# TensorE's queue in the order of the program text, in a kernel for one hybrid mixer and MLP layer

## The chip, the cores and the metric

The kernel runs on one core of one Trainium2 chip. Time is device time in microseconds (us) of one launch; the table below has the median of three runs, and the time of the one execution that the profiler recorded. The engines are TensorE (PE; its weight loads have their own row, PEld), VectorE (DVE), ScalarE (ACT), GpSimd (POOL) and SyncE (SP), which issues the DMAs. Each engine has a queue of its own and waits on semaphores of the others.

## What is computed

One layer on 2048 tokens of width 1024, in float32. Cut to what matters here:

```python
def hybrid_layer(x, ...):
    h = rmsnorm(x, norm_mix_w)
    proj = jnp.einsum("btd,dc->btc", h, w_in)              # 1024 -> 5648 columns
    u_b, u_c, u_h, z, xbc, dt_raw = jnp.split(proj, SPLITS, axis=-1)
    y_a = u_b * causal_dwconv(u_c * u_h, short_conv_w)     # short convolution mixer
    y_b = ssd_mixer(z, xbc, dt_raw, ...)                   # softplus(dt), chunked scan, gate, grouped rmsnorm
    x = x + jnp.einsum("btc,cd->btd", concat([y_a, y_b]), w_out)   # 2048 -> 1024
    h = rmsnorm(x, norm_mlp_w)
    hid = jnp.square(jax.nn.relu(jnp.einsum("btd,df->btf", h, w_up)))   # 1024 -> 4096
    return x + jnp.einsum("btf,fd->btd", hid, w_down)      # 4096 -> 1024
# and a last rmsnorm
```

In the scan, `dt` (16 heads) becomes a softplus, a cumulative sum over a chunk and exponentials of it; each chunk's output needs the state left by the chunk before.

## The kernel before

**Tiles.** Tokens lie on the free axis in blocks of 512 (`TB`), features on the 128 partitions; two blocks make a half. A float32 matmul is done as three matmuls on a high and a low part: `whi` and `wlo` of the weights, `uh` and `ul` of the data (L113 to L115 in `mm3`; L276 to L278 in `Seven.chain`). `Seven.chain` multiplies a 2 by 2 block of matrices with seven products in place of eight; the products accumulate in the PSUM banks `px`, `py` and `pw`, and between them ACT and DVE evict the banks (L727, L730, L874) and form the high and low parts of later data and weights (L100 and L101 for weights; L205, L206, L347 and L348 for data).

**Stages.** Norm and input projection of half 0, then half 1 with the scan of half 0 in between, then the output projection with the scan of half 1 in between, then the MLP up and down, then the last norm.

- `Rstd`: `reduce` sums squares with one-column matmuls into `pst` (L132), `root` makes the reciprocal root and two diagonals on ACT and DVE (L152), `spread` broadcasts them with two matmuls into `prb` (L178). The sums come from DVE (`facc`: L492 for the input norm, L1492 for the MLP's norm, L1079 for the last).
- `dt_part(b)` for block `b` (0 to 3): 16 or more matmuls `pd` (L625), an ACT copy `dts` (L629), four transposes `pt` (L633), then a chain of small DVE operations on 128x64 from L635 to L656 (with one ACT exponential), then two matmuls `pc` (L662, L663), a DVE copy (L664), a transpose `pr` (L671) and stores. The chain is, in its core:

```python
three(v) <- sum of pt; + bias; e = exp(-|v|)               # L635, L642, L643, L644
d = 1 / (e + 2); e = e * d; d = e * e; p = d / 17          # L646 to L650
for n in (15, 13, 11, 9, 7, 5, 3):
    nc.vector.scalar_tensor_tensor(out=p, in0=p, scalar=1.0 / n, in1=d, op0=ALU.add, op1=ALU.mult)
... L653, L655, L656: e = dt * a
```

- `Scan`: `load` brings a chunk's tiles (L1213 `dd`, L1218 `bc`, L1220 `xd`, L1222 `dec`), `front` transposes them (`ptx` L1253, `ptb` L1255 and L1256) and makes decays on ACT (L1267, L1268) and DVE (L1275), `back` does the matmuls `yo` (L1287), `st` (L1289), `yd` (L1292) and, later, a norm `pss` (L1317). `run` is a generator whose steps are interleaved with the products of the stage around it.
- `Output`: the output projection with `mm3`, 32 units; it adds the residual (L1478) and squares for the next norm (L1491, L1492).
- `Mlp`: up (evictions L871 to L878, the results go to DRAM by L861), then down, whose accumulators `acc` are loaded from DRAM (L978) and added to on DVE (L1018).

**What sets the order.** The kernel is written as one text. A scheduler runs over it ahead of the launch: it plays the program with estimated durations, and each engine takes of its instructions that are ready the one that it prefers. What comes out is a fixed list for each engine, and on the chip each engine works through its list in order, each instruction waiting for its semaphores. So an instruction that the text has early can stand later in an engine's list, and others ahead of it.

## Time and profile before

| | |
|---|---|
| median of 3 runs | 2664.36 us (2661.9 to 2666.43) |
| profiled execution | 2658.11 us |
| its span (first to last instruction) | 2656.4 us |
| DVE, ACT, POOL busy in it | 71%, 54%, 6% |
| DMA | 536.96 MB, mean 202 GB/s |
| mean granted TensorE clock | 0.995 |

A row of the page's first part gives an engine's busy time, its share of the span and its instructions. A row of the stretches gives for a window the busy time and, after x, the number of instructions of PE, PEld, DVE, ACT and POOL, then the granted TensorE clock, the DMA share and GB/s. A row of the timeline has start, duration, engine, line, operation, output and inputs, shapes and the number of like instructions that follow one another; at its end, in brackets, the idle time before it and what ended it. A row with a DMA and no start gives the tile, the number of transfers, their size and the time from issue to landing. Matmuls of 512 columns overlap: the distance of two starts tells more than the duration in their rows.

### The profile page before, as it was taken

How to read it: one execution, taken by the hardware profiler on the slowest of the kernel's cores; microseconds unless marked ns; L12 is line 12 of the kernel's file. 1: busy time of each engine (PE TensorE's matmuls, PEld its weight loads, DVE VectorE, ACT ScalarE, POOL GpSimd, SP SyncE). 2: the span in 40 equal slices, each digit the busy share in tenths (PEclk: the TensorE clock that was granted, in tenths of full speed). 3: DMA queues.
4: the chain of work that ended last, by engine and by line, in shares of the span. 5: the costliest groups of instructions: out<-in, count | busy, mean ns of one | idle time of the engine just before them, and what ended most of it. 6: DMA issues, size and time to landing. Idle time of an engine off the chain costs nothing.

```text
span 2656.4 us, 33528 instructions
## 1 busy us (share of the span) xinstructions
PE 2602.2 (98%) x12024; PEld 2124.8 (80%) x12024; DVE 1874.3 (71%) x2524; ACT 1436.5 (54%) x2178; POOL 146.1 (6%) x162
## 2 busy tenths in 40 slices
PE   7999999999999999998999999999999999999998
PEld 5788888778877888776888888888887888888887
DVE  7977867667667666666678675744447877888985
ACT  6654345766567566857336555755555434444443
POOL 0010000111111001111000000000000000000001
PEclk9999999999999999999999999999999999999999
DMA  3545735555555578867566786765558554665762
GB/s 145 196 174 182 278 143 202 182 152 174 169 161 168 165 262 267 254 200 232 193 208 214 258 315 254 258 234 178 209 183 297 155 152 153 206 219 165 249 209 71
DMA packets 292871, 536.96 MB, mean 202 GB/s; under 512 B 26208, under 2 KB 141920, under 8 KB 292704
## 3 DMA queue, kind: packets, MB, share of 16 engines
q1 hardware_dynamic: 292704, 534.82, 60.9%
q8 instruction: 94, 1.54, 0.2%
q14 instruction: 73, 0.60, 0.1%
HBM read 354.89 MB, written 179.83 MB: 201 GB/s over the span
## 4 chain that ended last, share of the span: by engine, by line
PE 59%; issue 26%; ACT 5%; DMA 4%; DVE 4%; POOL 1%; SPq 0%; POOLq 0%; DVEq 0%; ACTq 0%
PE px L276 9%; PE px L277 9%; PE px L278 9%; PE py L276 4%; PE py L277 4%; PE py L278 4%; PE pm L113 4%; PE pm L114 4%; PE pm L115 3%; PE pw L276 2%; PE pw L277 2%; PE pw L278 2%; ACT whi L100 1%; ACT dec L1267 1%; DMA dec<-rd_d 1%
## 5 line engine op out<-in xcount | busy, mean ns | idle before, releaser
L276 PE MATMUL px<-uh,whi 128*128 128x512 f32 x1672 | 657.7, 393 | 6.8 <-DVE acc L1018 1.8
L278 PE MATMUL px<-uh,wlo 128*128 128x512 f32 x1672 | 652.2, 390 | 0.0
L277 PE MATMUL px<-ul,whi 128*128 128x512 f32 x1672 | 651.9, 390 | 0.0
L276 PEld LDWEIGHTS px<-uh,whi 128*128 128x128 f32 x1672 | 314.5, 188 | 82.2 <-DVE acc L1018 3.2
L101 DVE TENSOR_TENSOR wlo<-wraw,whi 128x1024 fp32r<-128x1024 f32 x214 | 223.2, 1043 | 222.2 <-ACT whi L100 216.4
L278 PEld LDWEIGHTS px<-uh,wlo 128*128 128x128 f32 x1672 | 314.4, 188 | 66.4 <-issue 0.2
L277 PEld LDWEIGHTS px<-ul,whi 128*128 128x128 f32 x1672 | 314.6, 188 | 63.5
L100 ACT CAST whi<-wraw 128x1024 fp32r<-128x1024 f32 x214 | 193.6, 905 | 302.5 <-PE px L277 223.4
L276 PE MATMUL py<-uh,whi 128*128 128x512 f32 x836 | 327.4, 392 | 4.4 <-DVE acc L1018 3.4
L100 ACT CAST whi<-s 128x1024 fp32r<-128x1024 f32 x210 | 219.7, 1046 | 206.8 <-PE py L277 81.8
L277 PE MATMUL py<-ul,whi 128*128 128x512 f32 x836 | 325.6, 389 | 0.0
L278 PE MATMUL py<-uh,wlo 128*128 128x512 f32 x836 | 325.4, 389 | 0.0
L101 DVE TENSOR_TENSOR wlo<-s,whi 128x1024 fp32r<-128x1024 f32 x210 | 255.2, 1216 | 79.9 <-ACT whi L100 78.1
L113 PE MATMUL pm<-uh,whi 128*128 128x512 f32 (+1 forms) x648 | 253.1, 392 | 2.1 <-ACT uh L205 2.1
L114 PE MATMUL pm<-ul,whi 128*128 128x512 f32 (+1 forms) x648 | 249.9, 386 | 0.0
L115 PE MATMUL pm<-uh,wlo 128*128 128x512 f32 (+1 forms) x648 | 249.5, 385 | 0.0
L276 PEld LDWEIGHTS py<-uh,whi 128*128 128x128 f32 x836 | 156.9, 188 | 39.8 <-DVE acc L1018 3.8
L278 PEld LDWEIGHTS py<-uh,wlo 128*128 128x128 f32 x836 | 156.9, 188 | 33.0 <-DVE wlo L101 0.2
L277 PEld LDWEIGHTS py<-ul,whi 128*128 128x128 f32 x836 | 157.0, 188 | 32.0
L276 PE MATMUL pw<-uh,whi 128*128 128x512 f32 x418 | 163.5, 391 | 0.7 <-ACT pw L283 0.7
L347 ACT CAST uh<-rh 128x1024 fp32r<-128x1024 f32 (+1 forms) x128 | 120.3, 943 | 80.4 <-PE py L278 62.4
L278 PE MATMUL pw<-uh,wlo 128*128 128x512 f32 x418 | 162.9, 390 | 0.0
(232 smaller groups left out, 3763.2 us busy)
## 6 DMA issues: line engine op xcount, KB each, us to landing
hid_d<-e SPq DMA_DIRECT2D x96, 512.0 KB, 3.9
rh<-hid_d SPq DMA_DIRECT2D x96, 512.0 KB, 4.4
wraw<-w_in SPq DMA_DIRECT2D x68, 512.0 KB, 3.9
wraw<-w_down SPq DMA_DIRECT2D x104, 256.0 KB, 3.7
wraw<-w_up SPq DMA_DIRECT2D x48, 512.0 KB, 4.5
dec<-rd_d SPq DMA_DIRECT2D x32, 512.0 KB, 5.8
wraw<-w_out SPq DMA_DIRECT2D x32, 512.0 KB, 5.1
x_d<-xt SPq DMA_DIRECT2D x64, 256.0 KB, 3.2
```

Source lines behind the costliest of these rows:

```text
L100: nc.scalar.copy(hi, raw)
L101: eng.tensor_tensor(out=lo, in0=raw, in1=hi.bitcast(F32), op=ALU.subtract)
L113: nc.tensor.matmul(out, whi, hi, start=(k == 0), stop=False)
L114: nc.tensor.matmul(out, whi, lo, start=False, stop=False)
L115: nc.tensor.matmul(out, wlo, hi, start=False, stop=(k == nk - 1))
L276: nc.tensor.matmul(p, hi, h[0], start=not seeded and k == 0, stop=False, **kw)
L277: nc.tensor.matmul(p, hi, h[1], start=False, stop=False, **kw)
L278: nc.tensor.matmul(p, lo, h[0], start=False, stop=(k == len(g) - 1), **kw)
L347: nc.scalar.copy(p[i][0], t)
L1267: nc.scalar.activation(dec[:, i], dec[:, i], AF.Relu, bias=t["a"][:, i : i + 1], scale=-1.0)
```

## The change

The whole of `trunk` is traced in a context that keeps the instructions of the named engine in the order of the text. The other engines are still ordered by the scheduler, which now plays them against TensorE's fixed list.

```diff
     with tile.TileContext(nc) as tc:
-        trunk(tc, *args, out)
+        with tc.manual_schedule(engines={mybir.EngineType.PE}):
+            trunk(tc, *args, out)
```

No instruction is added or taken away. TensorE has 11512 instructions in both; 809 stand at another place, by up to 95 places, in 26 small stretches. The lists of DVE, ACT and SyncE change as well; GpSimd's is the same. Buffer numbers in tile names differ by two between the kernels.

First place, on TensorE: the matmuls of `dt_part(0)`, in the norm of block 1. `pd`, `pt`, `pc` and `pr` are those named above, `pm` the products of the input projection that follow. Before:

```order
L625 MATMUL pd<-uh_294,wdt 32x512
L625 MATMUL pd<-ul_295,wdt 32x512
L113 MATMUL pm<-uh_409,whi 128x512
L114 MATMUL pm<-ul_410,whi 128x512
L115 MATMUL pm<-uh_409,wlo 128x512
L113 MATMUL pm<-uh_409,whi 128x512
L633 MATMUL pt<-ident,dts 128x32 x4
L114 MATMUL pm<-ul_410,whi 128x512
L115 MATMUL pm<-uh_409,wlo 128x512
```

and 84 rows behind this `pt`:

```order
L113 MATMUL pm<-uh_469,whi 128x512
L662 MATMUL pc<-dts,tri 128x64
L663 MATMUL pc<-dts,ones_r 128x64
L114 MATMUL pm<-ul_470,whi 128x512
L115 MATMUL pm<-uh_469,wlo 128x512
L113 MATMUL pm<-uh_477,whi 128x512
L671 MATMUL pr<-ident,dts 64x128
```

After:

```order
L625 MATMUL pd<-uh_296,wdt 32x512
L625 MATMUL pd<-ul_297,wdt 32x512
L633 MATMUL pt<-ident,dts 128x32 x4
L662 MATMUL pc<-dts,tri 128x64
L663 MATMUL pc<-dts,ones_r 128x64
L671 MATMUL pr<-ident,dts 64x128
L113 MATMUL pm<-uh_411,whi 128x512
L114 MATMUL pm<-ul_412,whi 128x512
```

The four kinds stand directly behind one another, and the products that stood between `pt` and `pc` come behind `pr`. For block 1 it is the same: in the list of before 92 rows stand between its `pt` and its `pc`, in that of after none.

Second place, on TensorE: the first transposes of the scan (`ptx`, `ptb`), in the input projection of half 1; `px`, `py` are products of a pair of columns, `yo` the first matmuls of the chunk's `back`. Before:

```order
L276 MATMUL py<-uh_3717,whi 128x512
L1287 MATMUL yo<-bc,state_3777 128x128 x3
L1253 MATMUL ptx<-ident,xd 128x128 x4
L1255 MATMUL ptb<-ident,bc 128x128
L1256 MATMUL ptb<-bc 128x128
L1287 MATMUL yo<-bc,state_3777 128x128
L277 MATMUL py<-ul_3718,whi 128x512
```

After:

```order
L278 MATMUL py<-uh_3605,wlo 128x512
L1253 MATMUL ptx<-ident,xd 128x128 x4
L1255 MATMUL ptb<-ident,bc 128x128
L1256 MATMUL ptb<-bc 128x128
L276 MATMUL px<-uh_3655,whi 128x512
L277 MATMUL px<-ul_3656,whi 128x512
L278 MATMUL px<-uh_3655,wlo 128x512
```

The transposes moved ahead by 38 rows, from the middle of the next pair to its beginning. The scan's second start, in `Output`, has the same move by 30 rows.

Third place, on SyncE: the loads of that first chunk. `a` is a part of a weight (`a22` in `pairs`, L309), `rdt` the weights of dt. Before:

```order
L599 DMA rdt<-w_dt 128x128
L309 DMA a_3908<-w_in 128x512
L1213 DMA dd<-dt_d_105 128x256
L1218 DMA bc<-xs_d_97 128x128 x2
L1220 DMA xd<-xs_d_97 128x4x128
L1222 DMA dec<-rd_d_109 128x8x128
```

After:

```order
L599 DMA rdt<-w_dt 128x128
L1213 DMA dd<-dt_d_107 128x256
L1218 DMA bc<-xs_d_99 128x128 x2
L1220 DMA xd<-xs_d_99 128x4x128
L1222 DMA dec<-rd_d_111 128x8x128
L1243 DMA y<-sz_d_101 128x4x128
```

The load of `a` went behind the chunk's loads. At the scan's second start SyncE's list is the same in both.

## The prediction, made before the changed kernel ran

> **What bounds the kernel now.** I read the page first, then the stretches of 100 us, then the timeline at the places where the order of TensorE's instructions differs.
>
> ```profile
> PE 2602.2 (98%) x12024; PEld 2124.8 (80%) x12024; DVE 1874.3 (71%) x2524; ACT 1436.5 (54%) x2178; POOL 146.1 (6%) x162
> ```
>
> PE is busy for 2602.2 of 2656.4 us; DVE, the next engine, for 71%. A busy share can hide slow matmuls, so the number of matmuls per stretch matters too:
>
> ```profile
> 100.00:200.00 100.00, 100.00 (x443) 82.75 (x442) 78.89 (x94) 50.13 (x63) 9.40 (x12) 1.00 0.49 178
> 1200.00:1300.00 100.00, 91.72 (x456) 73.76 (x455) 62.83 (x94) 56.80 (x108) 12.23 (x9) 0.95 0.66 198
> 2000.00:2100.00 100.00, 93.17 (x398) 75.00 (x397) 81.86 (x108) 46.34 (x60) 0.00 (x0) 0.98 0.72 236
> ```
>
> The first row is the usual one: 443 matmuls in 100 us, one every 0.226 us, with no gap. PE idles visibly in few stretches; the two others shown lose 8 and 7 us. Hence two things: the same PE work can hardly run faster, since the unused time of PE is 2656.4 - 2602.2 = 54 us in all, the start and the tail included; and whatever makes PE wait anew is paid in full, because no other engine sets the end.
>
> **How I price a moved instruction.** The change keeps PE's work and moves 809 of its 11512 instructions, in small stretches. PE runs its queue in order, so a waiting instruction holds everything behind it. For each moved instruction I take from the trace of before (a) the time at which PE reached the place that the instruction now has (its slot), and (b) the time at which the last thing that it waits for was done. (b) minus (a), less a gap of before that vanishes there, is the new stall. It is a first-order figure: the other engines go on during a stall, which makes later stalls shorter, and their lists change too.
>
> **Start, +4.7.** The sum over block 1's squares (pst, L132) moves 27 places ahead.
>
> ```profile
> 32.55 0.39 PE L113 MATMUL pm<-uh,whi 128*128 128x512 f32 x1
> 33.98 3.08 DVE L492 TENSOR_TENSOR facc<-facc,sq 128x512 f32<-128x512 f32 x4
> ```
>
> Its slot is 32.55; DVE's last addition ends at 33.98 + 3.08 = 37.06. That is 4.5, and I put 0.2 on the broadcast (prb) behind it, whose chain over ACT and DVE now has only nine matmuls of cover. Bounds 2 and 6.
>
> **The dt chains, +35.6.** This is the largest term. In dt_part, pt, pc and pr are joined by a chain of 21 small DVE instructions (L635 to L656). The text gives PE nothing between pt and pc for blocks 0 and 1; the list of before puts 85 and 92 rows there.
>
> ```profile
> 50.26 0.43 PE L633 MATMUL pt<-ident,dts 32*128 32x32 f32 x4
> 53.75 0.28 DVE L635 TENSOR_REDUCE dts<-pt 128x64 f32<-128x128 f32 x1
> 69.20 0.22 DVE L656 TENSOR_TENSOR dts<-dts,hb 128x64 f32<-128x64 f32 x1
> 70.93 0.27 PE L671 MATMUL pr<-ident,dts 128*64 128x128 f32 x1
> ...
> 76.35 0.50 PE L276 MATMUL px<-uh,whi 128*128 128x512 f32 x1
> 85.02 0.68 DVE L209 TENSOR_TENSOR s<-wraw 128x512 f32<-128x512 f32 x1
> 85.62 0.54 DVE L647 RECIPROCAL dts<-dts 128x64 f32<-128x64 f32 x1
> 97.11 0.21 DVE L656 TENSOR_TENSOR dts<-dts,hb 128x64 f32<-128x64 f32 x1
> ...
> 523.77 0.39 PE L276 MATMUL py<-uh,whi 128*128 128x512 f32 x1
> 532.38 0.23 DVE L655 SCALAR_TENSOR_TENSOR dts<-dts 128x64 f32<-128x64 f32 x1
> 532.64 0.23 DVE L656 TENSOR_TENSOR dts<-dts,hb 128x64 f32<-128x64 f32 x1
> 533.01 0.41 PE L662 MATMUL pc<-dts,tri 128*128 128x64 f32 x2 [1.60 <-DVE dts L656]
> ```
>
> Block 0: PE is through with pt at 50.7 and pr could start at 70.93, so if DVE repeats itself PE stands still for 20.2. Bare, the chain takes 21 times 0.26 (the distance of the rows at 532.38 and 532.64) plus 0.3 for the longer reciprocal, 5.8, and with the hops to pt, pc and pr (about 1.5) 7.3. DVE's list of after still has 19 wide operations between L635 and L656 (21 before) at 0.60 each (85.02 to 85.62): 1.2 less than before; I take another 1.4 off since DVE should reach L635 earlier. That gives 17.6; bounds 7 and 20. Block 1: the list of after has six wide operations left inside the chain, so 5.8 + 6 x 0.60 = 9.4, and with the hops 11. If DVE is as late as before it is 97.32 - 76.35 = 21 plus 0.6 for pr; bounds 7 and 21.6. Block 3: pc's slot is 523.77, its release 532.87, less the gap of 1.99 that before has there (1.60 of it shown in the row): +7.0, bounds 3 and 9.
>
> **The scan's two starts, +13.9.** The transposes of the first chunk (ptx) stand ahead of a pair's products in the text, and some forty (first) and thirty (second) rows later in the list of before.
>
> ```profile
> 467.03 0.39 PE L276 MATMUL px<-uh,whi 128*128 128x512 f32 x1
> 473.54 0.50 PE L276 MATMUL px<-uh,whi 128*128 128x512 f32 x1 [0.91 <-ACT s L727]
> 473.91 0.43 SPq L1220 DMA_DIRECT2D xd<-xs_d  x1
> xd<-xs_d SPq DMA_DIRECT2D x1, 256.0 KB, 3.1
> ...
> 973.99 0.39 PE L113 MATMUL pm<-uh,whi 128*128 128x512 f32 x1
> 976.55 0.43 SPq L1220 DMA_DIRECT2D xd<-xs_d  x1
> xd<-xs_d SPq DMA_DIRECT2D x1, 256.0 KB, 5.5
> ```
>
> First start: slot 467.03, load landed at 473.91 + 3.1 = 477.0, so 10 late. But SyncE's list of after puts this load ahead of the weight load a22 (L309) that held it up in before, and it can be issued some 4.5 earlier: 5.4. The next products wait for an ACT eviction (L727) that now stands behind the chunk's eight decays: +2.6, less the 1.9 of gaps here that go (the wait at 473.54 among them): 6.0, bounds 2 and 12. Second start: slot 973.99, landing 976.55 + 5.5 = 982.05; SyncE's order is the same. 8.1 and 0.4 for the slower issue behind a store, less a gap of 0.6: +7.9, bounds 4 and 9.
>
> **Accumulator and eviction waits, +11.1.** Three places where the list of before has other products ahead of a waiting one, and the text has not.
>
> ```profile
> 1235.18 0.39 PE L113 MATMUL pm<-uh,whi 128*128 128x512 f32 x1
> 1242.68 0.69 DVE L1492 TENSOR_TENSOR facc<-sq,facc 128x512 f32<-128x512 f32 x1 [1.27 <-ACT sq L1491]
> 1243.42 0.80 PE L1317 MATMUL pss<-ssq,ones_r 128*128 128x128 f32 x2 [5.37 <-DVE facc L1492]
> ...
> 2008.69 0.39 PE L276 MATMUL px<-uh,whi 128*128 128x512 f32 x1
> 2012.37 0.68 DVE L874 TENSOR_TENSOR e<-py,s 128x512 f32<-128x512 f32 x1
> ...
> 2023.32 0.39 PE L276 MATMUL px<-uh,whi 128*128 128x512 f32 x1
> 2034.05 0.50 PE L276 MATMUL py<-uh,whi 128*128 128x512 f32 x1 [3.38 <-DVE acc L1018]
> 2034.93 0.69 DVE L1018 TENSOR_TENSOR acc<-px,acc 128x512 f32<-128x512 f32 x1 [0.94 <-DMA acc<-x_d]
> ```
>
> pss (L1317) stands 12 matmuls earlier, ahead of the same late release: 12 x 0.226 = +2.7. px at 2008.69 waits for an eviction (L874) that ended at 2012.45, 3.8 late, of which before lost 1.1: +2.7. At 2023.32 the text wants the next product, whose bank DVE frees at 2034.93 + 0.69 = 2035.62; before ran 25 later matmuls in that time, 25 x 0.226 = +5.7, work that is still to do when the bank comes free. Bounds of the three: 4 and 19.
>
> **Tail, +4.5.** The final norm's sums (pst) are asked for before their squares are added:
>
> ```profile
> 2621.44 0.28 PE L113 MATMUL pm<-uh,whi 128*128 128x256 f32 x1
> 2622.25 0.68 DVE L1079 TENSOR_TENSOR facc<-facc,sq 128x512 f32<-128x512 f32 x1
> ```
>
> Slot 2621.44, release 2622.93: 1.5; about as much for the broadcast behind it, and 1.5 for the same pair in the second half. Bounds 2 and 6.
>
> **Smaller places, +7.** Eight more moves (the dt of block 2, and single evictions) come out 0.4 to 2 us late each in the same way; an estimate, bounds 3 and 9.
>
> **The clock after a stall, +8.4.** PE does not resume at full rate:
>
> ```profile
> 1219.30 0.33 PE L1255 MATMUL ptb<-ident,bc 128*128 128x128 f32 x1 [2.92 <-DVE state L1303]
> 1220.37 0.63 PE L115 MATMUL pm<-uh,wlo 128*128 128x512 f32 x1
> ...
> 1245.94 0.63 PE L114 MATMUL pm<-ul,whi 128*128 128x512 f32 x1
> 1246.37 0.63 PE L115 MATMUL pm<-uh,wlo 128*128 128x512 f32 x1
> ```
>
> After the idle 5.37 us that end at 1243.42, matmuls start 0.43 apart in place of 0.226, and for about 3.8 us; a pause of 2.92 was enough for the same (0.63 at 1220.37). About seven matmuls at 0.20 more are 1.4 us; six of the stalls above are long enough and have no slow clock behind them in before (start, dt of blocks 0, 1 and 3, both scan starts): 8.4. Bounds 5 and 12.
>
> [...]
>
> **Sum.** 4.7 + 35.6 + 13.9 + 11.1 + 4.5 + 7 + 8.4 = 85.2. The profiled execution took 2658.1 (span 2656.4), so that one would become 2743. The runs shown have their median 6.3 above it, at 2664.4; I add the same and forecast **2750**.
>
> **The rivals.** (1) *The other engines use the stalls.* While PE stands still, DVE, ACT and the loads go on, so each stall shortens those behind it, and the chains run bare. Then each term sits at its lower bound: 2 + 7 + 7 + 3 + 2 + 4 + 4 + 2 + 3 + 5 = 39, **2703**. For it: DVE is idle 29% of the time. Against it: at dt of block 0 the wide operations are inside DVE's list, and DVE can't skip them.
> (2) *Nothing is absorbed.* Each term at its upper bound: 6 + 20 + 21.6 + 9 + 12 + 9 + 19 + 6 + 9 + 12 = 124, **2788**. For it: the new DVE and ACT lists were laid out against estimated durations, and what is late there holds PE again. Against it: 21.6 at block 1 needs wide operations that no longer stand in the chain.
> (3) *Faster: the text waits less than the list.* PE's own gaps in before are waits of instructions that the list put too early, 3.38 at 2034.05 for example. If text order moved these waits behind their releases, at the very most the 54 us that PE is unused could come back; with the bare chains of blocks 0 and 1 (14.6) still to pay, 2664 - 54 + 15 = **2625**. It decides only if more than 20 us of gaps go (the 14.6 and the 5 that can be told from none); at the three places shown the text moves the waiting instruction earlier, not later, which speaks against it.
> (4) *No difference.* 93% of PE's instructions keep their place; if all moved ones were ready, **2664**. Against it stand the 85 rows between pt and pc, which the text takes away.
>
> **How the numbers follow.** Forecast 0.60 (2720 to 2775), rival 1 0.20, rival 2 0.14, rivals 3 and 4 0.03 each. The range 2700 to 2785 leaves out rivals 3 and 4, most of rival 2 and the lower part of rival 1. A difference of 0.2%, 5 us, is about the least that a measurement of this kernel can tell from none. Faster by more: 0.03 (rival 3); within: 0.03 (rival 4); slower: 0.94 (the rest).
>
> **What would show it.** In the profile of the changed kernel the largest waits of PE should be pc for L656, 11 to 18 us each in the first 130 us, and the first stretch of 100 us should hold well under 300 matmuls (in before its row has x362); ptx should wait for xd at 470 and 980 of the old time, 5 and 8 us; px for L1018 once for over 8 us at the start of the down phase. The granted clock should dip behind each. If PE's wait for L656 in block 0 is under 9, rival 1 holds; if block 1's is over 18, rival 2. I am wrong in kind if the difference lies outside these places: if the list of DVE or ACT has PE wait a little in each of the many repeated steps, or if the dt waits are gone.

## The result, and the profile after

The changed kernel takes 2744.96 us (median of 4 runs, 2740.56 to 2746.54) where the kernel before, run beside it, takes 2664.0: a ratio of 1.0302 (95% interval 1.0286 to 1.0318), 81 us slower. Its profiled execution took 2740.56 us, 82.5 more than that of before. The forecast was 2750.

The page of the kernel after, its row of TensorE:

```profile
PE 2619.4 (96%) x12024; PEld 2137.8 (78%) x12024; DVE 1879.8 (69%) x2524; ACT 1436.4 (52%) x2176; POOL 141.2 (5%) x162
```

The span grew by 2738.9 - 2656.4 = 82.5 us. PE's busy time grew by 17.2 with the same instructions, its idle time by 65.3: most of the loss is waiting, and some is matmuls that ran slower. The stretches of 100 us of the kernel after (busy time and, after x, instructions of PE, PEld, DVE, ACT, POOL; then the granted clock, DMA share, GB/s) show where:

```profile
0.00:100.00 100.00, 63.85 (x248) 48.56 (x249) 71.36 (x136) 55.75 (x82) 2.86 (x11) 0.88 0.37 132
100.00:200.00 100.00, 90.83 (x399) 74.82 (x398) 67.34 (x97) 43.13 (x58) 6.33 (x8) 0.95 0.42 145
300.00:400.00 100.00, 100.00 (x443) 82.81 (x442) 79.96 (x98) 41.71 (x53) 7.87 (x12) 1.00 0.68 242
500.00:600.00 100.00, 82.14 (x387) 62.26 (x386) 57.97 (x108) 61.29 (x107) 5.86 (x9) 0.91 0.46 143
1000.00:1100.00 100.00, 90.92 (x444) 73.87 (x443) 62.13 (x89) 62.30 (x125) 8.82 (x6) 0.95 0.86 277
```

Three stretches are thinned that are full or nearly so in before: the first 120 us, 500 to 600 and 1000 to 1100 (the thin ones around 1300 and 2100 are there in before too, 65 to 75 us earlier). Between them (300 to 400 as the example) PE runs as before, 443 matmuls in 100 us. The waits of PE name the causes (waiter and what it waited for; us in all, times, the longest):

```profile
PE pc L662 <- DVE dts L656: 32.4, 3, 14.5
PE ptx L1253 <- DMA xd<-xs_d: 17.3, 3, 9.1
PE pst L132 <- DVE facc L492: 16.0, 2, 12.3
PE px L276 <- DVE acc L1018: 11.1, 10, 5.9
PE pss L1317 <- DVE facc L1492: 8.5, 1, 8.5
...
PE px L276 <- DVE e L874: 4.0, 1, 4.0
PE px L276 <- DVE eb L730: 3.7, 2, 1.9
```

The same view of before had 2.2 for pc, 0.6 for ptx, 12.7 for pst (block 0's, which the start needs in both) and 5.4 for pss. The dt of block 0 in the timeline of after:

```profile
57.89 0.40 PE L633 MATMUL pt<-ident,dts 32*128 32x32 f32 x4 [1.27 <-ACT dts L629]
58.34 0.29 DVE L635 TENSOR_REDUCE dts<-pt 128x64 f32<-128x128 f32 x1
72.43 0.23 DVE L656 TENSOR_TENSOR dts<-dts,hb 128x64 f32<-128x64 f32 x1
72.81 0.66 PE L662 MATMUL pc<-dts,tri 128*128 128x64 f32 x2 [14.52 <-DVE dts L656]
74.28 0.42 PE L671 MATMUL pr<-ident,dts 128*64 128x128 f32 x1 [0.39 <-DVE dts L664]
74.92 0.63 PE L114 MATMUL pm<-ul,whi 128*128 128x512 f32 x1
75.35 0.63 PE L115 MATMUL pm<-uh,wlo 128*128 128x512 f32 x1
...
112.12 0.77 PE L276 MATMUL px<-uh,whi 128*128 128x512 f32 x1
```

PE stands still from 58.3 to 72.8 while DVE works through the chain, then runs matmuls 0.43 apart. The first px behind dt of block 1 starts at 112.12; in before it started at 76.35. By that matmul the kernel has lost 35.8 us. Read in this way, start against start of one matmul in both timelines, the two executions drift apart by the steps in this table. The slow clock behind each wait is part of the drift, so the forecast's 1.4 for it is added at the six places where it was counted.

| place | forecast | drift |
|---|---|---|
| start, pst of block 1 | 4.7 + 1.4 | 7.2 |
| dt of block 0 | 17.6 + 1.4 | 18.1 |
| dt of block 1 | 11 + 1.4 | 10.7 |
| scan, first start | 6.0 + 1.4 | 7.8 |
| dt of block 3 | 7.0 + 1.4 | 8.2 |
| scan, second start | 7.9 + 1.4 | 11.2 |
| pss in the output projection | 2.7 | 4.1 |
| end of up, start of down | 2.7 + 5.7 | 6.2 |
| last norm | 4.5 | 2.4 |
| all the rest | 7 | 6.5 |
| sum | 85.2 | 82.4 |

### The profile page after: what moved, and what is told of

Its sections match the earlier page's. It is cut to its first block, busy times and chain, and to the rows that moved or that the text cites. A ratio compares the mean times of both kernels' runs of the same rounds, so it can differ in the third digit from the quotient of the medians.

```text
span 2738.9 us, 33543 instructions
## 1 busy us (share of the span) xinstructions
PE 2619.4 (96%) x12024; PEld 2137.8 (78%) x12024; DVE 1879.8 (69%) x2524; ACT 1436.4 (52%) x2176; POOL 141.2 (5%) x162
## 4 chain that ended last, share of the span: by engine, by line
PE 57%; issue 26%; DVE 6%; DMA 5%; ACT 4%; POOL 1%; SPq 0%; POOLq 0%; DVEq 0%; ACTq 0%
PE px L276 9%; PE px L277 9%; PE px L278 8%; PE py L276 4%; PE py L277 4%; PE py L278 4%; PE pm L113 3%; PE pm L114 3%; PE pm L115 3%; PE pw L276 2%; PE pw L278 2%; PE pw L277 2%; DMA dec<-rd_d 2%; ACT whi L100 1%; PE yd L1292 1%
## 5 line engine op out<-in xcount | busy, mean ns | idle before, releaser
L277 PE MATMUL pw<-ul,whi 128*128 128x512 f32 x418 | 162.7, 389 | 0.0
```

The lines of the kernel that those rows point to most:

```text
L277: nc.tensor.matmul(p, hi, h[1], start=False, stop=False, **kw)
```

## The experiments

My theory: the loss is made place by place, by single instructions at the head of PE's queue that are not ready, each with a stall and a slow clock behind it. The rivals: the loss comes from the new lists of the other engines over the whole kernel; or waits that are taken away come back elsewhere. All ratios below are against the kernel before, run beside each kernel.

### Text order in some stages only

For these three the whole-kernel context goes, and `text_order()` is the same context, put around stages.

```diff
-            ws = proj.start()
+            with text_order(): ws = proj.start()
```

> TensorE in text order only while the first stage (norms, first blocks of the projection, dt of blocks 0 and 1) is traced; the scheduler orders it in the rest. Theory (the loss is made place by place, by waits at the head of TensorE's queue): the two profiles drift apart by 7.2 us up to the first dt matmul and by 18.1 more at dt of block 0; at dt of block 1 the region ends, so products of the next stage may stand between pt and pc (36 rows, 8.1 us of the 9.8 us wait). 7.2 + 18.1 + 2 = 27 us above before: 2691 us. Rival (the loss comes from the other engines' lists, which change over the whole kernel): within 10 us of before, or as slow as a proportional share of the whole, under 2680 us.

Measured: 2688.79 us, 26.6 above before (2662.18), ratio 1.0097 (1.0082 to 1.0112); pc of block 0 waits 14.5 as in the whole change.

The complement has the same context around `first_half`, `second_half`, the loops over the output's units, and the MLP, and not around `start`.

> The complement: TensorE in text order in every stage but the first. Theory: what the profiles drift apart behind the first stage, 82.4 - 36.1 = 46 us: 2710 us, with the waits for xd (8 and 9 us), pc of block 3 (9.5) and pss (9) as in the changed kernel and no wait for L656 in the first 130 us. Rival (not additive, an early stall gives the other engines a lead that hides later ones): clearly more than 46 us.

Measured: 2706.08 us, 43.9 above before, ratio 1.016 (1.0145 to 1.0175). Both sizes are as the drift says. Their sum is 26.6 + 43.9 = 70.5; with the 8 us of block 1's pc that neither kernel has, it comes near the whole 81. The loss adds up over stages.

```diff
+    with text_order():
+        with tc.tile_pool(name="up", ...) as mlp.up:
             ...
+        mlp.down(c4, ws)
```

> TensorE in text order only in the MLP's up and down and the last norm. Theory: 82.4 - 68.5 = 14 us: 2678 us, most of it at the end of the up phase (px waiting for L874) and in the last norm. Rival (the small differences in the down phase are noise or come from earlier stages): 8 us or less, 2672 us.

Measured: 2672.1 us, 9.9 above before, ratio 1.0036 (1.0024 to 1.0048): between the two, nearer the rival. Some 4 us of the 14 that I had put down to the MLP are not made there when it alone is in text order; by the interval it is 1 to 8.

### What the slow clock costs

```diff
+    def fill_wait(bank, n):
+        for _ in range(n):
+            k = bank.shape[-1] // P
+            out = bank.rearrange("p (k c) -> p k c", k=k)
+            nc.tensor.matmul(out, ones_r, ones_r.unsqueeze(1).to_broadcast([P, k, P]), start=True, stop=True)
...
             pc = psum("tp", "pc", 2)
+            fill_wait(pc[:, 128:512], (74, 42, 0, 44)[b])
```

> The changed kernel with matmuls on constants, whose results nobody reads, ahead of five waiting instructions: 74, 42 and 44 of 384 columns ahead of pc of blocks 0, 1 and 3, 28 and 34 of 512 columns ahead of the first ptx of the scan's two halves. They end before the wait does, so TensorE is busy in place of idle. Theory (a pause of some 3 us or more halves the clock for about 4 us, 1.4 to 1.9 us lost each): five slow stretches less, 7 to 9 us below the changed kernel, 2737 us, with the granted clock at full in these places. Rival (the slow stretch costs nothing, since TensorE then waits for less): no difference, 2745 us; rival (the added matmuls delay the waiting ones): above 2748 us.

The kernel also had 10 such matmuls ahead of block 1's pst, a sixth place that the expectation does not count. Measured: 2733.72 us, ratio 1.0272 (1.0252 to 1.0293) against 1.0302 (1.0286 to 1.0318) for the change: 232 matmuls more, and some 8 us less. The intervals overlap a little, so the size is loose; the profiled executions lie 6.7 us apart. The stretches behind the waits, first of the changed kernel (dt of block 0, dt of block 3, second start of the scan):

```profile
72.00:78.00 6.00, 4.81 (x16) 3.90 (x17) 3.14 (x9) 1.84 (x4) 0.00 (x0) 0.58 0.47 129
580.00:586.00 6.00, 5.16 (x15) 4.29 (x16) 2.00 (x8) 0.75 (x3) 0.00 (x0) 0.53 0.26 66
1037.00:1043.00 6.00, 5.48 (x17) 4.61 (x18) 1.49 (x3) 4.95 (x15) 0.00 (x0) 0.50 0.99 263
```

then the same places with the waits filled:

```profile
72.00:78.00 6.00, 5.54 (x19) 4.43 (x20) 2.66 (x7) 1.78 (x4) 0.00 (x0) 0.72 0.54 138
578.00:584.00 6.00, 4.60 (x23) 3.73 (x23) 2.80 (x11) 1.89 (x5) 0.48 (x2) 1.00 0.33 89
1033.00:1039.00 6.00, 6.00 (x30) 4.97 (x30) 1.49 (x3) 5.11 (x15) 0.00 (x0) 1.00 1.08 275
```

At the second and third place the clock column goes from 0.53 and 0.50 to 1.00, and at the first start of the scan it is 1.00 as well. At the three places in the first stage it fell all the same, to 0.72 to 0.79 over 6 to 8 us. There 1.46 us of idle time were left ahead of block 0's pc, 1.94 ahead of block 1's and 2.11 ahead of pst, and ahead of the two pr the changed kernel has 0.39 and 0.38 more; at block 3, 1.40 were left and the clock stayed at 1.00. So three of the five expected slow stretches went, not five; at these three places the matmuls of 512 columns had lost 3.6 us in the changed kernel by starts 0.43 apart. Filling a wait brings time back, then, but that the total came out as the theory had it is in part luck, and where the rest of the 8 us comes from these runs do not show.

### The dt chains

Here the whole kernel is in text order again, and the text is changed: the generator of `dt_part` is advanced from inside the products that follow (`with_dt` takes a step of `held` in the next group).

```diff
                     self.bias()
-                    for _ in dts:
-                        next(work, None)
+                    next(dts)
                     for _ in work:
                         pass
-                    work = self.begin_sums()
+                    held = dts
...
+                    work = with_dt(self.begin_sums())
...
+                    if m == 0 and name in ("b21", "t3", "t4"):
+                        next(self.dt_left, None)
...
+            if self.h:
+                for _ in range(4):
+                    yield
             pc = psum("tp", "pc", 2)
```

> TensorE in text order over the whole kernel, as in the change, but dt_part's steps stand apart in the text: between pt and pc of block 0 the 72 products of the next group and its pd, of block 1 the first five products of the first pair, of blocks 2 and 3 four more products. Theory (the three long waits for L656 are lost because the text has no work between pt and pc): 18.1 + 10.7 + 0.7 + 8.2 = 38 us come back, 2707 us, no wait of pc over 2 us. Rival (text order as such costs, whatever the text; the other engines' lists are to blame): 2735 us or more.

Measured: 2704.82 us, 42.3 above before (2662.55), ratio 1.016 (1.0145 to 1.0175); no wait of pc is left among PE's waits. Between the ratios 1.0302 and 1.016 lie 38 us, as many as were expected. The text, not the act of keeping it, made these stalls.

The other side of the same question, DVE's order inside the chain:

```diff
-            ws = proj.start()
+            with tc.manual_schedule(engines={mybir.EngineType.DVE}): ws = proj.start()
```

> The changed kernel, with DVE too in text order in the first stage, so that nothing stands between the 21 operations of the dt chain of blocks 0 and 1 on DVE. Theory (the waits of 14.7 and 9.0 us are the chain, 5.8 us, and the wide operations in it at 0.60 us each): both waits fall to 6 to 7 us, 8 and 2.5 us less, 2734 us if DVE's text order costs nothing elsewhere in the stage. Rival (the chain itself takes that long, each operation waiting for the one ahead): the waits stay at 14 and 9 us.

Measured: 2752.72 us, ratio 1.034 (1.0325 to 1.0356): slower than the change. The timeline of this kernel, block 0 and then block 1:

```profile
68.80 0.28 DVE L635 TENSOR_REDUCE dts<-pt 128x64 f32<-128x128 f32 x1
71.48 1.78 DVE L652 SCALAR_TENSOR_TENSOR dts<-dts 128x64 f32<-128x64 f32 x7
73.92 0.22 DVE L656 TENSOR_TENSOR dts<-dts,hb 128x64 f32<-128x64 f32 x1
74.30 0.66 PE L662 MATMUL pc<-dts,tri 128*128 128x64 f32 x2 [7.23 <-DVE dts L656]
...
106.03 0.28 DVE L635 TENSOR_REDUCE dts<-pt 128x64 f32<-128x128 f32 x1
114.92 0.22 DVE L652 SCALAR_TENSOR_TENSOR dts<-dts 128x64 f32<-128x64 f32 x1
115.06 0.68 DVE L380 TENSOR_TENSOR facc<-facc,lx 128x512 f32<-128x512 f32 x1
115.66 0.21 DVE L652 SCALAR_TENSOR_TENSOR dts<-dts 128x64 f32<-128x64 f32 x1
118.87 0.22 DVE L656 TENSOR_TENSOR dts<-dts,hb 128x64 f32<-128x64 f32 x1
119.15 0.69 PE L662 MATMUL pc<-dts,tri 128*128 128x64 f32 x2 [15.51 <-DVE dts L656]
```

In block 0 the chain is bare: seven L652 in 1.78 us, 0.25 each, and 74.14 - 68.80 = 5.3 us for all of it. The wait halves, from 14.52 to 7.23. In block 1 wide operations of the next stage (L380 among them), which this region does not bind, came in between, 0.74 from one L652 to the next, and the wait grew from 8.8 to 15.5. So the wide operations inside the chain set its length, in both directions. The sizes agree across three chains: with 19 wide operations (block 0 of the change) it takes 14.3 us, with 21 (block 0 of before) 15.7, with 16 (block 1 here) 13.1. Less the bare 5.3, that is 0.47 to 0.49 for each, an estimate from these rows. The total came out above the expected 2734, because DVE's text order also made pst of block 1 wait 9.25 us, some 5.5 more than in the change, block 1's pc 6.7 more, and a weight's low part come 2.6 late.

### The starts of the scan, and the first norm

```diff
             self.load_rows(begin)
-            yield
+            for _ in range(5 if self.bufs == 1 else 6):
+                yield
...
+            for _ in range(2 * bb):
+                yield
             st.reduce(acc)
...
             def hook(at):
-                for _ in range(1 + at % 2):
+                for _ in range(1 + at % 2 + (at in (20, 30, 40, 50, 60))):
                     next(side, None)
```

The edits of the kernel with dt apart are in it too. The last lines give the scan, which now starts later in the output projection, five extra steps further on; so more than its start moves.

> As the kernel with dt_part's steps apart, and further: the first transposes of the scan's two halves stand four and five steps later in the text, and the sum of squares of block 1 (pst) and its broadcast (prb) some steps later. Theory: 7.8 + 11.1 + 7.2 = 26 us more come back, 2681 us; what stays is the output projection's pss, two evictions, the end of the up phase and the last norm. Rival (waits are only pushed to the next place): within 8 us of the kernel with dt_part's steps apart.

Measured: 2698.23 us, ratio 1.0133 (1.0117 to 1.015), 6.6 less than the kernel with dt apart: the rival. The control, the same text with the scheduler ordering PE:

> The same mended text, but TensorE ordered by the scheduler as in the kernel before: the control. Theory (the text's order matters only where it is kept): no difference from before, 2664 us within 5. Rival (the mended text is itself faster, or slower): 2655 us or less, or 2672 us or more.

Measured: 2674.22 us, ratio 1.0046 (1.0031 to 1.0061): the mended text costs 12 us where the order isn't even kept. Something in it is bad by itself. I then took the two edits apart: dt and pst without the later scan,

> TensorE in text order over the whole kernel; dt_part's steps stand apart in the text, and block 1's sum of squares (pst) and its broadcast (prb) come some steps later; the scan is as in the change. Theory (the first norm's wait of 5 us is lost because the text asks for the sum too early): 7 us less than with dt_part's steps apart alone, 2698 us. Rival (the time of the kernel with the whole text mended, 2698 us, came from pst alone, and shifting the scan gave nothing, or the wait moves to pc of block 0, 3.6 us there): the same number, so it is the comparison with the next run that tells; a wait of 3 us or more at pc of block 0 here would speak for 2702 us.

measured 2701.93 us, ratio 1.0144 (1.0124 to 1.0163): some 3 us less than with dt apart, not 7, which by the intervals can hardly be told from none; and pc of block 0 waits 3.2 as the rival has it. Then I made the scan later by whole periods, which I thought would keep its steps clear of the products' evictions (again with extra steps in `hook`):

```diff
-            yield
+            for _ in range(8 if self.bufs == 1 else 7):
+                yield
...
-                for _ in range(1 + at % 2):
+                for _ in range(1 + at % 2 + (at >= 80)):
```

> As the kernel with dt_part and pst mended, and the scan is later by whole periods: by seven steps (one pair of columns) in its first half, by six steps (two units of the output projection) in its second, so that its steps keep their phase against the products around them. Theory (shifting the scan by four and five steps gave nothing because it changed that phase in all 32 chunks; the waits for xd themselves can be had back): both waits for xd of the first chunks go and no other wait of ptx, st or pss grows over 2 us, some 16 us less than with dt and pst mended, 2682 us. Rival (any later scan only moves the waits): 2695 us or more.

Measured: 2696.31 us, ratio 1.0128 (1.0107 to 1.015), 5.6 less than with dt and pst mended (the intervals overlap), where 16 to 20 were expected: the theory falls. The waits of PE without the later scan,

```profile
PE ptx L1279 <- DMA xd<-xs_d: 15.7, 3, 7.9
...
PE pss L1343 <- DVE facc L1518: 8.9, 1, 8.9
...
PE st L1315 <- DVE stmp L1299: 2.3, 4, 1.0
...
PE px L276 <- ACT pw L283: 0.6, 1, 0.6
```

and with it (the eviction's line is L751 here, L727 in the kernel before):

```profile
PE pss L1343 <- DVE facc L1519: 11.5, 3, 4.4
PE st L1315 <- DVE stmp L1299: 5.8, 2, 4.2
PE px L276 <- ACT s L751: 4.9, 5, 1.6
...
PE px L276 <- ACT pw L283: 2.9, 2, 2.4
...
PE ptx L1279 <- ACT dts L697: 2.2, 1, 2.2
```

The wait for the load, 15.7 us, is gone whole; 2.6 of pss, 3.5 of st, 4.9 and 2.3 of evictions and 2.2 of ptx came in its place, 15.5 together. Over all rows of the view the sum falls by 3.5 only, from 78.0 to 74.5. Pairs are of different kinds, so a shift by one pair is no return to the same neighbours. With the scheduler ordering PE the same shift costs too:

> The kernel before (TensorE ordered by the scheduler) with the scan later by the same whole periods and nothing else changed. Theory (with the phase kept a later scan costs nothing, unlike the shift by four and five steps, which cost 12 us with the scheduler too): 2663 us within 4. Rival (a later scan costs by itself): 2670 us or more.

Measured: 2668.31 us, ratio 1.0019 (1.0007 to 1.003), some 5 us: between the theory (2667 at most) and the rival (2670 at least), and so for neither. What costs this is not settled: the later place itself, the neighbours that it gives the steps, or the extra steps in `hook`, which no run has alone. The runs show only that the waits spread over ACT's evictions, st and pss.

So the starts needed a test that leaves the scan where it is. The last kernel keeps the text of before and lets the scheduler order PE in three stretches: `start`, the first five pairs of `second_half` and the first three units of the output projection. The rest is in text order.

```diff
+                if m == 5: kept.enter_context(text_order())
...
-            for n in range(45):
+            for n in range(3):
                 proj_out.unit(n, hook)
...
+            with text_order():
+                for n in range(3, 45):
+                    proj_out.unit(n, hook)
```

> TensorE in text order but for three stretches, which the scheduler orders: the first stage, the first five pairs of the second half (the scan's first start, dt of blocks 2 and 3), and the first three units of the output projection (the scan's second start). Nothing of the text is changed, so the scan keeps its place. Theory (the change loses 64 of its 82 us in these stretches): 36.1 + 16.7 + 11.1 = 64 us less than the changed kernel, 18 us above before, 2681 us, with no wait of ptx or pc over 2 us. Rival (as where the scan was made later: what is had back at its starts is lost again behind them): 2695 us or more.

Measured: 2677.42 us, 17.0 above before (2660.46), ratio 1.0053 (1.0034 to 1.0072), where 18 were expected. Set beside the kernel with text order in all stages but the first (43.9 above), freeing the other two stretches alone gives 27 us back, where their drift is 7.8 + 8.2 + 11.2 = 27. Those stalls are made there, and they can be had back without being paid elsewhere. No version beat the kernel before.

## Why the prediction was right

**The bound.** PE was at 98% in before, and 65.3 of the 82.5 us lost are new idle time of PE. That moving 809 of 11512 instructions costs 3%, with the order of the other 10703 kept, fits this bound: what the other engines get done during a stall does not end the kernel earlier, unless it shortens a later wait of PE.

**Slot against release.** Taking the place's time in before and the release's time in before gave each of the six larger places to within 2 us (table). It worked best where the release hangs on nothing that PE does meanwhile (the second start's load, the chain on DVE). One of the six came out by luck, the scan's first start (below).

**The dt chains.** 35.6 was forecast for blocks 0, 1 and 3. Measured idle time of PE: 14.5 ahead of block 0's pc, 8.8 ahead of block 1's and 9.1 ahead of block 3's, of which before has 1.6; and 1.3 at pt and 0.4 at each of two pr, 33 together. The wide operations left in DVE's list, 19 and 6, were counted rightly, and they were the right thing to count. The sizes were a little off. The text has 19 small operations on DVE from L635 to L656 and one on ACT, not 21 on DVE; the bare chain took 5.3 where 5.8 was put, and a wide operation added 0.47 to 0.49 where 0.60 was put. Block 0's chain began at once behind pt (58.29 to 58.34), 3 us sooner than in before, where 1.4 was allowed. So block 1's wait, 8.8, lies below the 11 to 18 that the prediction named as a sign, though its rivals' signs did not come either (under 9 at block 0, over 18 at block 1). In the run with a bare chain block 0's wait was 7.2, near the lower bound.

**The scan's starts.** 7.7 and 9.1 of wait for xd were measured. The second is the 8.1 + 0.4 of the forecast and 0.6 more; its drift is 2 more than the forecast. At the first the net 6.0 was right, but its parts were not. The forecast had 5.4 for the load and 2.6 for an ACT eviction (L727), less 1.9 of gaps. After:

```profile
508.40 0.43 SPq L1220 DMA_DIRECT2D xd<-xs_d  x1
xd<-xs_d SPq DMA_DIRECT2D x1, 256.0 KB, 6.0
...
514.40 1.11 PE L1253 MATMUL ptx<-ident,xd 128*128 128x128 f32 x4 [7.72 <-DMA xd<-xs_d]
521.45 0.57 ACT L727 COPY s<-px 128x512 f32<-128x512 f32 x1
522.10 0.47 PE L276 MATMUL px<-uh,whi 128*128 128x512 f32 x1
```

The load was issued some 5 us earlier against PE's slot, as forecast (4.5), but it took 6.0 us to land, not the 3.1 of before; and the eviction ended at 522.02, just in time for the px at 522.10, which shows no wait. An error of +2.3 and one of -2.6 cancel, and that is luck.

**The step that was mis-sized: the start of the down phase, +5.7.** I held the release of the accumulator's bank fixed at its time in before, and counted the 25 matmuls done ahead of it as work still to do. The timeline of after:

```profile
2097.95 0.39 PE L278 MATMUL pw<-uh,wlo 128*128 128x512 f32 x1
2103.52 0.69 DVE L1018 TENSOR_TENSOR acc<-px,acc 128x512 f32<-128x512 f32 x1 [0.47 <-DMA acc<-x_d]
2104.27 0.80 PE L276 MATMUL px<-uh,whi 128*128 128x512 f32 x1 [5.92 <-DVE acc L1018]
```

PE waits 6.1 us beyond the usual distance (5.92 of it idle, where the prediction had named over 8 as a sign), not the 12.3 of the slot in before (2023.32 to 2035.62). The gaps of before that went there, 3.4 and three smaller ones, come to 4.9 together, so about 1 us of idle time is new, and the place's drift is 0.3. The accumulators' loads were issued some 5.5 us earlier against PE's own position (2098.71, 0.5 behind the slot; 2029.37 in before, 6 behind it). They stand behind stores of the up phase that wait for DVE (3.2 us in all from 2080 to 2100), and DVE had just had a wait of PE of 4.0 us (for L874) to get ahead. This reading of the cause is from the trace alone, and no run tests it; with the MLP alone in text order the same two waits are 6.4 and 3.7 us, so they do not hang on the stalls of the earlier stages. It is what rival 1 says of all places; it held at this one. The term at the end of up was too small: 2.7 forecast, 5.9 measured, since a slow clock follows there too (2.4 us by starts 0.43 apart), which I had not counted. That the two errors, 5.4 too much and 3.2 too little, cancel in part is luck again.

**The slow clock.** I counted six stretches of 1.4. Over the kernel, matmuls of 512 columns lost 24.3 us in after and 13.0 in before by starts 0.43 apart in place of 0.227: 11.3, against 8.4 forecast. About 7 of it is at the six places that I had counted (only 0.4 at the scan's first start), the rest mainly behind a wait for L730 (1.7) and at the end of up (2.4). I had looked for stalls as long as the pause of 2.92 us that had a slow stretch behind it in before; in after shorter ones had one too, but not each time. The two waits for L730 left PE idle for 1.84 us (until 265.93) and 1.87 us (until 496.63); the stretches around them in after:

```profile
264.00:270.00 6.00, 4.16 (x19) 3.35 (x19) 5.80 (x8) 1.61 (x2) 0.00 (x0) 1.00 0.22 87
...
493.00:500.00 7.00, 5.13 (x16) 3.76 (x15) 7.00 (x8) 5.51 (x7) 0.00 (x0) 0.78 0.89 307
```

The clock stayed at 1.00 behind the first and fell behind the second.

**The rivals.** The first (every term at its lower bound, 2703) and the second (at its upper, 2788) both lie 40 us off. The third needed gaps of before to close by 20 us; the drift falls back by 1 to 1.6 us at a time in a few places.

**The offset.** The runs of after have their median 4.4 above the profiled execution; I had added 6.3, as in before. With 85.2 for 82.4 that makes the 5 us between forecast and result.

## What to carry to other kernels

Where one engine is near 100%, as here, an order for it is as good as its worst few places: find each instruction that the new order brings forward, take the time of its new place and the time of its last input from the old trace, and add a slow-clock allowance for each long pause (in the changed kernel 0.4 to 2.4 us each behind pauses of 1.87 to 14.52 us). Add up the parts one by one, and compare them one by one afterwards: a sum can be right with wrong parts. Text order cost little here in a stage whose text already has work between a producer and its consumer on another engine, and was expensive where a chain, a load or a reduction is written straight ahead of its use. A later start takes a wait away only at that place; where two streams of work share the engines behind it, look at all waits of the stage before counting the gain.

## What was not expected of the hardware

Pauses of under 2 us cost clock in some places here and not in others: 1.87 us did and 1.84 us did not in the two rows above, and with the waits filled a rest of 1.46 us ahead of pc of block 0 (ahead of its pr the changed kernel has 0.39 more) was followed by a granted clock of 0.72 over 6 us, a rest of 1.40 us at block 3 by 1.00. What decides between them is open. And 232 matmuls on constants, put into the waits, did not make the kernel slower but faster, by some 8 us with a loose interval.
